# HGRN2 level products of one head: full 128-token blocks, or pairs of 64-column strips

## The chip, the core and the metric

The program runs on one core of a Trainium2 chip. TensorE (PE in the profile, with its weight loads as PEld) multiplies matrices from SBUF into PSUM, VectorE (DVE) and ScalarE (ACT) read and write both, GpSimd (POOL) works in SBUF and issues transfers, and SyncE (SP) issues transfers. Each engine takes its own instructions strictly in a written order and waits on semaphores for the others. The metric is the device time of one execution in microseconds.

## The reference, cut to what matters

Two layers run over 1024 latent tokens (width 1024) behind 256 context tokens. The first mixes neighbourhood attention and mLSTM, and the change does not touch it. The second has 16 bidirectional HGRN2 heads with keys and values of width 128. For one head and one direction:

```
f = lb + (1 - lb) * sigmoid(f_pre);  k = 1 - f;  lf = log(f);  q = silu(q_pre)
b = cumsum(lf)                                          # inside a chunk
o = (q * exp(b)) @ S + sum over s <= t of (q_t . (exp(b_t - b_s) * k_s)) v_s
S = exp(b_last) * S + (k * exp(b_last - b))^T @ v       # carried to the next chunk
```

Both directions are summed, normalised per head, multiplied by silu(z) and projected out. The state S starts from the context tokens.

## The kernel before, in words

Matrix products with weights are made from operands split into a high and a low part, three products each (`dense`, L128 to L130). These carry most of the time of TensorE. In the HGRN2 stage the channels of a head lie on the 128 partitions and tokens run along the columns.

For a head, `hg_proj` makes the forget gates F of both directions and q; `hg_intra` makes the 128 x 128 matrix A of each block of 128 tokens, which holds the weight of token s for token t in both directions; `hg_vz` makes the values v and the gate z, in groups of 24 dense matmuls; `hg_close` transposes the decayed keys; `hg_ctx` makes the starting states from the context; `hg_scan` carries the states over the eight blocks, forms the output of each block from A, q and the states (L1088 to L1090, into PSUM tile acc), and after each four blocks takes the root mean square (squares on ACT at L1104, the power on POOL at L154 and L156) and scales and gates into z (DVE, L1108); `hg_out` transposes z (L1148) and stores it. `wo_sums` and `y_diff` are side work on POOL: they load, add and store pieces of the output weights and of earlier results.

A is built by levels. At level l, with h = 2^l, each pair of neighbouring blocks of h tokens needs the products between its two halves: keys are decayed up to the border between them, queries from it. K and Q hold the keys and queries decayed so far, for both directions; after each level the two halves are multiplied by the totals T of the neighbouring block (DVE, L1048), and the totals are multiplied pairwise (L1050). For the product ACT copies the keys of the right direction into ksel (L1023), TensorE multiplies 128-token blocks (L1028), and DVE writes the part under the level's mask into A (L1037). Everything is done for the two halves of 512 tokens in turn, each with its own tiles. Level 0 and the diagonal are made otherwise: `hg_near` multiplies keys and queries elementwise on DVE, and `hg_close` sums over the channels with a matrix of ones (L998, L999) after a split into two parts, and copies the result to A under a mask (L1001).

What sets the order: the program is written head by head, and a planner with its own costs then lays out each engine's instructions, so that dense products of the next head stand between the level products of this one. The order on each engine is fixed when the kernel is built. PSUM has two banks for dense products (mm), three for level products and states (s), two for transposes (tr) and one for the output (acc). The gate z has one buffer: the next head's z can be written only when this head's transposes have read it, and until then the banks of the dense products that hold it stay in use.

Of the kernel before, what the change touches and what calls it, by code (L numbers as in the profile page):

```python
# [9 lines left out]
F32 = mybir.dt.float32  # L10
# [34 lines left out]
class Prog:  # L45
# [836 lines left out]
    def hg_proj(self, h, pool, w=None):  # L882
# [4 lines left out]
        F = [self.t(p, [P, 2, 512], F32, "gF", 1) for p in (pool, self.fp)]  # L887
# [6 lines left out]
        for d, t0, n in todo:  # L894
            w[d] = w[d] or self.wring([col(1 + d)], P)
            ps = self.ps("mm", [P, n])
            self.proj_tr(ps, w[d], 0, t0, n)
            dst = Fc[:, d, :] if t0 == LAT else F[t0 // 512][:, d, :]
            nc.scalar.activation(dst, ps, AF.Sigmoid)
            nc.vector.tensor_scalar(out=dst, in0=dst, scalar1=olb, scalar2=lb, op0=ALU.mult, op1=ALU.add)  # L900
# [67 lines left out]
    def hg_intra(self, st, pool):  # L968
        nc = self.nc
        n = 512  # L970
        hv = {}
        for hf in (1, 0):
            F, q = st["F"][hf], st["q"][hf]
            K = self.t(pool, [P, 2, n], F32, "gK", 2)
            nc.vector.tensor_scalar(out=K, in0=F, scalar1=-1.0, scalar2=1.0, op0=ALU.mult, op1=ALU.add)
            Q = self.t(pool, [P, 2, n], F32, "gQ", 2)
            for d in range(2):
                nc.vector.tensor_tensor(out=Q[:, 1 - d, :], in0=q, in1=F[:, d, :], op=ALU.mult)
            A = self.t(pool, [P, 4, P], F32, "gA", 2)
            hv[hf] = dict(Q=Q, A=A, T=F, K=K)  # L980
# [7 lines left out]
    def hg_close(self, hv, pool):  # L988
        nc = self.nc
        for i in range(2):  # L990
            for hf in (1, 0):
                H = hv[hf]
# [3 lines left out]
                pa = self.ps("s", [P, 4, P])  # L996
                p2 = pa.rearrange("p a b -> p (a b)")
                nc.tensor.matmul(p2, lhsT=self.ones, rhs=hi, start=True, stop=False)  # L998
                nc.tensor.matmul(p2, lhsT=self.ones, rhs=lo, start=False, stop=True)  # L999
                mask = self.ident8 if i else self.lmask0  # L1000
                nc.vector.copy_predicated(H["A"], mask.unsqueeze(1).to_broadcast([P, 4, P]), pa)  # L1001
        for hf in (1, 0):
            H = hv[hf]
            H["kn"] = []
            for d in range(2):
                p = self.ps("tr", [P, 4, P])
                for c in range(4):
                    nc.tensor.transpose(p[:, c, :], H["K"][:, d, c * P : (c + 1) * P], self.ident)
                k_ = self.t(pool, [P, 512], F32, "gkn", 4).rearrange("p (a b) -> p a b", a=4)
                nc.scalar.copy(k_, p)  # L1010
                H["kn"].append(k_)


    def hg_level(self, H, lev, pool):
        nc = self.nc
        n, h = 512, 1 << lev
        nb = n // (2 * h)
        K, Q, A, Tt = H["K"], H["Q"], H["A"], H["T"]

        pick = lambda t: _skew(t[:, 0, :].rearrange("p (b s i) -> p b s i", s=2, i=h), 2, n)  # L1020
        if lev > 0:
            ksel = self.t(pool, [P, n], F32, "gksel", 3)
            nc.scalar.copy(ksel.rearrange("p (b s i) -> p b s i", s=2, i=h), pick(K))  # L1023
            qp = pick(Q)
            pa = self.ps("s", [P, 4, P])
            nbc = P // (2 * h)
            for c in range(4):
                nc.tensor.matmul(  # L1028
                    pa[:, c, :].rearrange("p (b s i) -> p b s i", s=2, i=h),
                    lhsT=ksel[:, c * P : (c + 1) * P], rhs=qp[:, c * nbc : (c + 1) * nbc], start=True, stop=True,  # L1030
                )
            mask = self.lmask[:, lev - 1, :].unsqueeze(1).to_broadcast([P, 4, P])
            if lev == 1:

                nc.vector.tensor_tensor(out=A, in0=pa, in1=mask, op=ALU.mult)
            elif lev < 6:
                nc.vector.copy_predicated(A, mask, pa)  # L1037
            else:
                nc.scalar.copy(A[0:64, :, 64:P], pa[0:64, :, 64:P])
                nc.scalar.copy(A[64:P, :, 0:64], pa[64:P, :, 0:64])  # L1040
# [8 lines left out]
        Tn = self.t(pool, [P, 2, nb], F32, f"gT{lev}", 2)  # L1049
# [3 lines left out]


    def hg_near(self, H, q, pool):
        nc = self.nc
        n = 512
        K, Q = H["K"], H["Q"]

        kx = bass.AP(K.tensor, K[:, 1, 1:n].offset, [list(K.ap[0]), [2, n // 2], [-(n + 1), 2]])  # L1060
        qx = bass.AP(Q.tensor, Q.offset, [list(Q.ap[0]), [2, n // 2], [n + 1, 2]])
        pr = [self.t(pool, [P, n], F32, "gkn", 4) for _ in range(2)]
        nc.vector.tensor_tensor(out=pr[0].rearrange("p (b s) -> p b s", s=2), in0=kx, in1=qx, op=ALU.mult)
        nc.vector.tensor_tensor(out=pr[1], in0=K[:, 0, :], in1=K[:, 1, :], op=ALU.add)
        nc.vector.tensor_tensor(out=pr[1], in0=pr[1], in1=q, op=ALU.mult)
        H["near"] = pr

    def hg_scan(self, st, halves, S, pool):
# [4 lines left out]
        for c in range(7, 0, -1):  # L1073
            H = halves[c // 4]
            u = self.ps("s", [P, P])
            nc.tensor.matmul(u, lhsT=H["kn"][1][:, c % 4, :], rhs=v[:, c, :], start=True, stop=True)
# [547 lines left out]
```

## Time and profile before

| | us |
|---|---|
| median of 3 runs | 3482.13 (3481.38 to 3482.68) |
| the profiled execution, first to last instruction | 3480.9 |
| PE busy | 3431.2 (99%) |
| PEld busy | 3042.3 (87%) |
| DVE busy | 2307.4 (66%) |
| ACT busy | 1488.6 (43%) |
| POOL busy | 725.6 (21%) |

The profile is of one execution on the hardware. A group of instructions is given with its line, engine, operation, output tile, input tiles, shapes and count; the idle time before it is put down to what ended it. Matmuls are pipelined and their recorded ends are modelled, so starts are the better measure of how long one holds TensorE. A shape "128*64" of a matmul means 128 rows and 64 columns of weights, and "128x128" the moving data. A line of the timeline has the start, the time to the end of its last instruction, and how many instructions it holds.

### The profile page before, as it was taken

The numbers are of one execution on the slowest core, as the hardware profiler recorded it, in microseconds if no ns is written. First come the engines' busy times: TensorE is split into PE (matmuls) and PEld (weight loads), VectorE is DVE, ScalarE is ACT, GpSimd is POOL, SyncE is SP. The second block draws the span as 40 slices with busy tenths as digits, with TensorE's granted clock in tenths as the row PEclk, the third lists the DMA queues.
The fourth block names the chain that finished last, engine by engine and source line by source line (L and its number), as shares of the span: only waits on it lengthen the run. The fifth ranks groups of instructions, "written<-read, shape, count | busy, mean of one in ns | idle before, by whom it ended". The sixth has DMA issues, their size and how long they took to land.

```text
span 3480.9 us, 60852 instructions
## 1 busy us (share of the span) xinstructions
PE 3431.2 (99%) x22668; PEld 3042.3 (87%) x22668; DVE 2307.4 (66%) x5447; ACT 1488.6 (43%) x3577; POOL 725.6 (21%) x1076
## 2 busy tenths in 40 slices
PE   8999999999999999999999999999999999999997
PEld 5779998889989888898888999999999999999876
DVE  4546665666655566787666676667677677666767
ACT  5445554554544444455354333333333333333442
POOL 2222222222111112221110122122223222111125
PEclk9999999999999999999999999999999999999999
DMA  5542222322233434444752111111112211111274
GB/s 205 173 132 59 81 76 74 91 79 75 79 87 99 147 117 127 133 128 148 223 158 68 49 58 55 56 58 58 58 55 64 64 59 57 41 34 34 83 233 154
DMA packets 331527, 333.34 MB, mean 96 GB/s; under 512 B 30984, under 2 KB 277960, under 8 KB 331232
## 3 DMA queue, kind: packets, MB, share of 16 engines
q1 hardware_dynamic: 291008, 222.76, 21.7%
q0 software_dynamic: 40224, 106.69, 9.0%
q8 instruction: 179, 2.93, 0.4%
q14 instruction: 116, 0.95, 0.1%
HBM read 259.40 MB, written 69.79 MB: 95 GB/s over the span
## 4 chain that ended last, share of the span: by engine, by line
PE 89%; DVE 3%; issue 3%; DMA 2%; ACT 1%; POOL 1%; SPq 0%; POOLq 0%; ACTq 0%; DVEq 0%
PE mm L128 18%; PE mm L129 18%; PE mm L130 18%; PE s L1028 5%; PE mm L835 3%; PE mm L836 3%; PE mm L837 3%; PE acc L775 2%; PE tr L755 2%; PE acc L547 2%; PE s L556 2%; PE acc L537 1%; PE acc L1090 1%; PE acc L1088 1%; PE acc L1089 1%
## 5 line engine op out<-in xcount | busy, mean ns | idle before, releaser
L129 PE MATMUL mm<-hl,wh 128*128 128x512 f32 (+1 forms) x1600 | 587.1, 367 | 0.0
L128 PE MATMUL mm<-hh,wh 128*128 128x512 f32 (+1 forms) x1600 | 584.3, 365 | 0.0
L130 PE MATMUL mm<-hh,wl 128*128 128x512 f32 (+1 forms) x1600 | 583.7, 365 | 0.0
L128 PE MATMUL mm<-wh,hh 128*128 128x256 f32 (+1 forms) x1520 | 471.2, 310 | 1.2 <-ACT ev L317 0.6
L129 PE MATMUL mm<-wl,hh 128*128 128x256 f32 (+1 forms) x1520 | 469.9, 309 | 0.0
L130 PE MATMUL mm<-wh,hl 128*128 128x256 f32 (+1 forms) x1520 | 469.0, 309 | 0.3 <-DVE hl L262 0.3
L130 PEld LDWEIGHTS mm<-hh,wl 128*128 128x128 f32 x1600 | 301.6, 189 | 45.0 <-issue 0.5
L128 PEld LDWEIGHTS mm<-hh,wh 128*128 128x128 f32 x1600 | 301.4, 188 | 44.6 <-issue 0.3
L129 PEld LDWEIGHTS mm<-hl,wh 128*128 128x128 f32 x1600 | 301.6, 189 | 43.7 <-issue 0.2
L128 PE MATMUL mm<-wzh,hh 128*128 128x256 f32 x1024 | 299.7, 293 | 2.3 <-DVE gq L909 1.4
L128 PEld LDWEIGHTS mm<-wh,hh 128*128 128x128 f32 x1520 | 286.5, 189 | 16.0 <-issue 1.1
L129 PEld LDWEIGHTS mm<-wl,hh 128*128 128x128 f32 x1520 | 286.5, 188 | 14.7 <-issue 3.0
L130 PEld LDWEIGHTS mm<-wh,hl 128*128 128x128 f32 x1520 | 286.4, 188 | 13.8 <-issue 1.5
L130 PE MATMUL mm<-wzh,hl 128*128 128x256 f32 x1024 | 292.3, 285 | 0.0
L129 PE MATMUL mm<-wzl,hh 128*128 128x256 f32 x1024 | 292.0, 285 | 0.0
L72 ACT CAST wh<-wraw 128x512 fp32r<-128x512 f32 x240 | 147.3, 619 | 233.0 <-PE mm L129 175.8
L73 DVE TENSOR_TENSOR wl<-wraw,wh 128x512 fp32r<-128x512 f32 x240 | 164.8, 691 | 89.6 <-ACT wh L72 80.4
L1023 ACT COPY gksel<-gK 128x512 f32<-128x512 f32 x192 | 120.0, 633 | 218.2 <-PE s L1028 127.3
L1028 PE MATMUL s<-gQ,gksel 128*128 128x128 f32 x1536 | 203.9, 276 | 0.4 <-ACT gksel L1023 0.4
L128 PEld LDWEIGHTS mm<-wzh,hh 128*128 128x128 f32 x1024 | 193.4, 189 | 3.8 <-DVE gq L909 2.4
L129 PEld LDWEIGHTS mm<-wzl,hh 128*128 128x128 f32 x1024 | 193.6, 189 | 0.0
L130 PEld LDWEIGHTS mm<-wzh,hl 128*128 128x128 f32 x1024 | 192.7, 188 | 0.0
(400 smaller groups left out, 8017.5 us busy)
## 6 DMA issues: line engine op xcount, KB each, us to landing
wraw<-in_wab_dram SPq DMA_DIRECT2D x112, 256.0 KB
wraw<-in_wc_dram SPq DMA_DIRECT2D x96, 256.0 KB
wraw<-yd SPq DMA_DIRECT2D x94, 256.0 KB
adar<-in_wada_dram POOLq DMA_DIRECT2D x32, 512.0 KB, 4.4
wraw<-in_wc_dram SPq DMA_DIRECT2D x128, 128.0 KB
md<-ev POOLq DMA_DIRECT2D x60, 256.0 KB, 2.8
mloz<-md SPq DMA_DIRECT2D x40, 256.0 KB
adar<-in_wada_dram SPq DMA_DIRECT2D x16, 512.0 KB
```

The source lines that it names most:

```text
L72: nc.scalar.copy(hi, x)
L73: nc.vector.tensor_tensor(out=lo, in0=x, in1=hi.bitcast(F32), op=ALU.subtract)
L128: mm(ps, lhsT=lh(k), rhs=rh(k), start=(start and k == 0), stop=False)
L129: mm(ps, lhsT=lh(k), rhs=rl(k), start=False, stop=False)
L130: m = mm(ps, lhsT=ll(k), rhs=rh(k), start=False, stop=(stop and k == nk - 1))
L547: nc.tensor.matmul(num, lhsT=qc[:, j, :], rhs=C[d][:, j, :], start=False, stop=(j == 1))
L556: nc.tensor.matmul(u, lhsT=st["k"][c][:, j * P : (j + 1) * P], rhs=vw, start=True, stop=True)
L835: mm(ps, lhsT=yh[k], rhs=w.h(kk), start=(kk == 0), stop=False)
L836: mm(ps, lhsT=yh[k], rhs=w.l(kk), start=False, stop=False)
L837: mm(ps, lhsT=yl[k], rhs=w.h(kk), start=False, stop=(kk == 8 * len(qs) - 1))
L1023: nc.scalar.copy(ksel.rearrange("p (b s i) -> p b s i", s=2, i=h), pick(K))
L1028: nc.tensor.matmul(pa[:, c, :].rearrange("p (b s i) -> p b s i", s=2, i=h), lhsT=ksel[:, c * P : (c + 1) * P], rhs=qp[:, c * nbc : (c + 1) ...
```

## The change

All 1024 tokens of a head are now one piece, with one tile each for F, K, Q and ksel (1024 columns, one buffer) and one chain of levels. Level products are made in blocks of 64 tokens: 64 keys as weights times 64 queries, two such products side by side in the two column halves of TensorE (`strip`, with its tile position), so that the results of 16 blocks fill one PSUM bank of 512 columns. They are gathered in D (128 x 8 x 64) under masks of 64 columns; at level 6, which joins the two 64-token blocks of a pair, D and the level's product are copied into A. The diagonal and level 0, which were elementwise products and column sums with ones, become two more such products: the diagonal of (K0 + K1) with q, and level 0 like the others. `hg_near`, the ones and two masks are gone.

```diff
-        F = [self.t(p, [P, 2, 512], F32, "gF", 1) for p in (pool, self.fp)]
+        F = self.t(self.fp, [P, 2, LAT], F32, "gF", 1)
...
     def hg_intra(self, st, pool):
...
+        K = self.t(pool, [P, 2, LAT], F32, "gK", 1)
+        nc.vector.tensor_scalar(out=K, in0=F, scalar1=-1.0, scalar2=1.0, op0=ALU.mult, op1=ALU.add)
+        Q = self.t(pool, [P, 2, LAT], F32, "gQ", 1)
+        ks = [self.t(pool, [P, 512], F32, "gkn", 4) for _ in range(2)]
         for hf in (1, 0):
...
+            nc.vector.tensor_tensor(out=ks[hf], in0=K[:, 0, s], in1=K[:, 1, s], op=ALU.add)
             for d in range(2):
-                nc.vector.tensor_tensor(out=Q[:, 1 - d, :], in0=q, in1=F[:, d, :], op=ALU.mult)
...
-            self.hg_near(hv[hf], q, pool)
+                nc.vector.tensor_tensor(out=Q[:, 1 - d, s], in0=q[hf], in1=F[:, d, s], op=ALU.mult)
...
+        pa = self.ps("s", [P, 8, 64])
+        for c in range(8):
+            for b in range(2):
+                o = c % 4 * P + b * 64
+                self.strip(pa[:, c, :], b, ks[c // 4][:, o : o + 64], q[c // 4][:, o : o + 64])
+        nc.vector.tensor_tensor(
+            out=hv["D"], in0=pa, in1=self.lmask[:, 0, :].unsqueeze(1).to_broadcast([P, 8, 64]), op=ALU.mult
+        )
         for lev in range(7):
-            for hf in (1, 0):
-                self.hg_level(hv[hf], lev, pool)
+            self.hg_level(hv, lev, pool)
...
+    def strip(self, out, b, lhsT, rhs):
+        s = slice(b * 64, (b + 1) * 64)
+        self.nc.tensor.matmul(out[s], lhsT=lhsT, rhs=rhs, start=True, stop=True, tile_position=(0, b * 64))
...
-    def hg_close(self, hv, pool):
-                hi = self.t(pool, [P, 512], F32R, "gsg", 1)
-                lo = self.t(pool, [P, 512], F32R, "gyt", 1)
-                self.split(hi, lo, H["near"][i])
...
-                nc.tensor.matmul(p2, lhsT=self.ones, rhs=hi, start=True, stop=False)
-                nc.tensor.matmul(p2, lhsT=self.ones, rhs=lo, start=False, stop=True)
...
     def hg_level(self, H, lev, pool):
-        n, h = 512, 1 << lev
+        n, h = LAT, 1 << lev
...
-            ksel = self.t(pool, [P, n], F32, "gksel", 3)
-            nc.scalar.copy(ksel.rearrange("p (b s i) -> p b s i", s=2, i=h), pick(K))
...
-            for c in range(4):
-                nc.tensor.matmul(
-                    pa[:, c, :].rearrange("p (b s i) -> p b s i", s=2, i=h),
-                    lhsT=ksel[:, c * P : (c + 1) * P], rhs=qp[:, c * nbc : (c + 1) * nbc], start=True, stop=True,
-                )
...
+        ksel = self.t(pool, [P, n], F32, "gksel", 1)
+        nc.scalar.copy(ksel.rearrange("p (b s i) -> p b s i", s=2, i=h), pick(K))
+        pa = self.ps("s", [P, 8, 64])
+        for c in range(8):
+            for b in range(2):
...
+                self.strip(out, b, ksel[:, o : o + 64], rhs)
...
+            if lev == 6:
+                nc.scalar.copy(A[s, :, s], D[s])
+                nc.scalar.copy(A[s, :, e], pa[s])
+        if lev < 6:
+            nc.vector.copy_predicated(D, self.lmask[:, lev + 1, :].unsqueeze(1).to_broadcast([P, 8, 64]), pa)
...
-        Tn = self.t(pool, [P, 2, nb], F32, f"gT{lev}", 2)
+        Tn = self.t(pool, [P, 2, nb], F32, f"gT{lev}", 1)
```

The planner lays the instructions out anew in the whole HGRN2 stage; ahead of it and behind it the order stays. In the changed kernel the line numbers shift: its strips are L997, the output products L1073 to L1075 (before L1088 to L1090), the scaling L1093 (L1108), the output transposes L1133 (L1148), the predicated copy L1042 (L1037), the updates of K and Q L1050 (L1048).

On PE, at the end of a head's scan, the four transposes of the second half of its output (tile tr, from gz) stand in the middle of the head behind it. Before, 56 dense matmuls stand between the last output product and this piece:

```order
L128 MATMUL mm_28096<-wzh_27988,hh_20674 128x256
L1148 MATMUL tr_27783<-ident_77,gz_27077 128x128
L924 MATMUL tr_28038<-ident_77,gEc_28036 128x128 x2
L1148 MATMUL tr_27783<-ident_77,gz_27077 128x128
L129 MATMUL mm_28096<-wzl_27987,hh_20674 128x256
L1148 MATMUL tr_27783<-ident_77,gz_27077 128x128
L130 MATMUL mm_28096<-wzh_27988,hl_20675 128x256
```

Now the same transposes, with 22 dense matmuls between the last output product and the strips of level 0:

```order
L130 MATMUL mm_29002<-wzh_28894,hl_20672 128x256
L997 MATMUL s_28724<-gQ_28693,gksel_28722 64x64 x16
L1133 MATMUL tr_28663<-ident_77,gz_27990 128x128
L924 MATMUL tr_28944<-ident_77,gEc_28942 128x128 x2
L1133 MATMUL tr_28663<-ident_77,gz_27990 128x128 x3
L997 MATMUL s_28748<-gQ_28693,gksel_28746 64x64 x16
L128 MATMUL mm_29056<-wzh_28894,hh_20671 128x256
```

The transposes now stand between the strips of level 0 and those of level 1, with no dense matmul among them; nine heads have this piece.

On DVE at the same place, before, the scaling of the output (into gz) stands among the first steps of the half that is not yet at its levels:

```order
L1048 TENSOR_TENSOR gQ_27813<-gQ_27813,gT_5708_27835 128x2x128x2
L978 TENSOR_TENSOR gQ_27824<-gq_27771,gF_27516 128x512 x2
L1063 TENSOR_TENSOR gkn_27828<-gK_27822,gQ_27824 128x512
L1064 TENSOR_TENSOR gkn_27829<-gK_27822 128x512
L1108 SCALAR_TENSOR_TENSOR gz_27077<-acc_27479,gss_27504,gz_27077 128x128 x4
L1048 TENSOR_TENSOR gQ_27824<-gQ_27824,gF_27516 128x2x256
```

Now, with the copy of level 0 (L1042) and the update of Q by level 0 (L1050) behind it:

```order
L979 TENSOR_TENSOR gQ_28693<-gq_28622,gF_28397 128x512 x2
L979 TENSOR_TENSOR gQ_28693<-gq_28651,gF_28397 128x512 x2
L949 TENSOR_SCALAR gq_29193<-gFc_28398 128x512
L1093 SCALAR_TENSOR_TENSOR gz_27990<-acc_28360,gss_28385,gz_27990 128x128 x4
L1042 COPY_PREDICATED gD_28702<-glm_4352_20630,s_28724 128x512
L1050 TENSOR_TENSOR gQ_28693<-gQ_28693,gF_28397 128x2x512
```

All of Q now passes level 0 behind the scaling, where before one half was a level ahead.

On POOL, in the eleventh head, the norm's two steps (gss) stand near the end of two weight sums. Before:

```order
L1125 TENSOR_TENSOR gEc_31552<-gEc_31552,gknc_31551 128x256
L1131 DMA sw_12_74<-gknc_31551 128x256
L1125 TENSOR_TENSOR gEc_31552<-gEc_31552 128x256
L1131 DMA sw_13_75<-gEc_31552 128x256
L1131 DMA sw_14_76<-gEc_31552 128x256
L154 TENSOR_SCALAR gss_31213<-gss_31213 128x4
L156 TENSOR_TENSOR gss_31213<-gss_31213,mhalf_82 128x4
```

Now:

```order
L1110 TENSOR_TENSOR gEc_31478<-gEc_31478,gknc_31477 128x256
L1116 DMA sw_12_74<-gknc_31477 128x256
L154 TENSOR_SCALAR gss_31140<-gss_31140 128x4
L1110 TENSOR_TENSOR gEc_31478<-gEc_31478 128x256
L1116 DMA sw_13_75<-gEc_31478 128x256
L156 TENSOR_TENSOR gss_31140<-gss_31140,mhalf_82 128x4
L1116 DMA sw_14_76<-gEc_31478 128x256
```

The first step of the norm moved ahead of the last sum and its two stores, the second ahead of the last store. Three of the first four output transposes then stand on PE right behind the strips of the diagonal, 124 rows of dense and fp32 products after the context product L961 and those 16 strips.

More of the change, by code (lines that the diff above doesn't have):

```diff
@@ L1048, in hg_level, with hg_scan @@
             nc.vector.tensor_tensor(out=v, in0=v, in1=tot, op=ALU.mult)
-        Tn = self.t(pool, [P, 2, nb], F32, f"gT{lev}", 2)
+        Tn = self.t(pool, [P, 2, nb], F32, f"gT{lev}", 1)
         nc.vector.tensor_tensor(out=Tn, in0=Tv[:, :, :, 0], in1=Tv[:, :, :, 1], op=ALU.mult)
         H["T"] = Tn
[L1055 to L1068, printed above, removed]
+    def hg_scan(self, st, H, S, pool):
         nc = self.nc
@@ L1073, in hg_scan @@
         for c in range(7, 0, -1):
[L1074 removed]
             u = self.ps("s", [P, P])
[L1076 removed]
+            nc.tensor.matmul(u, lhsT=H["kn"][c // 4][1][:, c % 4, :], rhs=v[:, c, :], start=True, stop=True)
             s = self.t(pool, [P, P], F32, "gS1", 10)
             nc.vector.scalar_tensor_tensor(
[L1079 removed]
+                out=s, in0=sb[c], scalar=H["T"][:, 1, c : c + 1], in1=u, op0=ALU.mult, op1=ALU.add
             )
```

80 lines of the change are left out of this document (31 added, 49 removed).

## The prediction

> **What bounds the kernel now.** I read the page first, then the busy time of each engine by stretches, then the groups by line, then the timeline of the places that the change touches.
>
> ```profile
> span 3480.9 us, 60852 instructions
> PE 3431.2 (99%) x22668; PEld 3042.3 (87%) x22668; DVE 2307.4 (66%) x5447; ACT 1488.6 (43%) x3577; POOL 725.6 (21%) x1076
> PEclk9999999999999999999999999999999999999999
> ```
>
> TensorE is busy 99% of the span at full granted clock. A busy TensorE need not be at its peak, but it waits for almost nobody. The HGRN2 stage runs from about 1885 to 3340 us, one head in 90 us; this is one head (columns: stretch, length, then busy time of PE, PEld, DVE, ACT, POOL, clock, DMA share, GB/s):
>
> ```profile
> 2174.00:2264.00 90.00, 90.00 (x628) 83.51 (x627) 62.99 (x121) 32.21 (x76) 18.59 (x27) 1.00 0.18 57
> ```
>
> PE is busy all 90.00 us, DVE 62.99, ACT 32.21, POOL 18.59. So what this stage loses or gains is PE's own work, plus any wait that PE did not have before. The groups that the change touches:
>
> ```profile
> L1028 PE MATMUL s<-gQ,gksel 128*128 128x128 f32 x1536 | 203.9, 276 | 0.4 <-ACT gksel L1023 0.4
> L998 PE MATMUL s<-gsg,ones 128*128 128x512 f32 x64 | 26.6, 415 | 0.0
> L999 PE MATMUL s<-gyt,ones 128*128 128x512 f32 x64 | 25.5, 399 | 0.0
> L1048 DVE TENSOR_TENSOR gK<-gK,gT 128x512 f32<-128x512 f32 x192 | 151.7, 797 | 8.5 <-ACT gksel L1023 8.4
> L1048 DVE TENSOR_TENSOR gQ<-gQ,gT 128x512 f32<-128x512 f32 x192 | 133.3, 694 | 14.3 <-PE s L1028 14.2
> L1023 ACT COPY gksel<-gK 128x512 f32<-128x512 f32 x192 | 120.0, 633 | 218.2 <-PE s L1028 127.3
> ```
>
> The program has 48 level products a head, 768 in all; the trace has 1536 matmuls on L1028. One fp32 product is two records, and prices must be counted in records. What a record occupies is read from the starts:
>
> ```profile
> 2102.22 1.05 PE L1028 MATMUL s<-gQ,gksel 128*128 128x128 f32 x8
> 2103.11 1.04 PE L1008 MATMUL tr<-ident,gK 128*128 128x128 f32 x8
> 2109.53 0.39 PE L128 MATMUL mm<-hh,wh 128*128 128x512 f32 x1
> 2109.76 0.40 PE L129 MATMUL mm<-hl,wh 128*128 128x512 f32 x1
> ```
>
> Eight records take 2103.11 - 2102.22 = 0.89 us, 0.111 each (0.222 an fp32 product); a 512-column matmul of split operands takes 0.23.
>
> **Removed from PE.** 1536 x 0.111 = 170.5 us of level products and 128 x 0.23 = 29.4 us of column sums with the ones (L998, L999): 199.9 us.
>
> **Added to PE.** Eight levels (seven and the diagonal) of 16 strips in 16 heads: 2048 fp32 products of 64 weight columns by 64 moving columns. The nearest row is the attention's product of values, which puts two 64-column strips beside each other in the same way, with 128 moving columns:
>
> ```profile
> 806.50 0.28 PE L130 MATMUL mm<-wh,hl 128*128 128x256 f32 x1
> 806.62 0.28 PE L128 MATMUL mm<-wh,hh 128*128 128x256 f32 x1
> 806.83 0.44 PE L775 MATMUL acc<-apT,avw 128*64 128x128 f32 x4
> 807.10 0.61 PE L775 MATMUL acc<-apT,avc 128*64 128x128 f32 x8
> 807.53 0.61 PE L775 MATMUL acc<-apT,avw 128*64 128x128 f32 x8
> 808.07 0.75 PE L755 MATMUL tr<-ident,aP 128*96 128x128 f32 x5
> 808.58 0.36 PE L707 MATMUL s<-akh,aqs 128*128 128x256 f32 x1
> 808.78 0.28 PE L708 MATMUL s<-akl,aqs 128*128 128x256 f32 x1
> 808.90 0.29 PE L718 MATMUL s<-akh,aqs 128*128 128x264 f32 x1
> 806.83 0.20 PEld L775 LDWEIGHTS acc<-apT,avw 128*64 128x64 f32 x4
> 806.99 0.25 PEld L775 LDWEIGHTS acc<-apT,avc 128*64 128x64 f32 x4
> ```
>
> Eight records from 807.10 to 807.53 are 0.054 each, 0.109 a strip: half of the 0.222 of a full-width product, for half of its work. With 64 moving columns the price lies between 0.109 (nothing gained from fewer columns) and 0.055 (half). The full-width product has weights as wide as its moving data and keeps the rate of one of them, so I go near the lower end; but twice as many instructions must start in a given time as in any row here, so I take 0.060. Sum: 2048 x 0.060 = 122.9 us, and 223.2 at the upper end.
>
> A block of strips has a price of its own. From 806.62 to 808.90 are 2.28 us. The work in it is three matmuls of 256 columns (0.12 each, 806.50 to 806.62), ten strips (1.09) and five transposes (0.10 to 0.11 each): 1.95 to 2.00. So 0.28 to 0.33 us are lost where PE goes over to strips and back; I take 0.30. In the order of the changed kernel the strips stand in 148 blocks, eight to a head and some 20 more because transposes stand between the strips of level 0 in six heads: 148 x 0.30 = 44.4 us. The Trainium skill, "TensorEngine Tiling (Array Packing)", section Key Properties, says that a change of tiling mode drains TensorE, which speaks against short blocks; the 0.28 to 0.33 us agree with it, and a sum that left it out would come 44 us lower.
>
> PE's work: 122.9 + 44.4 - 199.9 = -32.6 us.
>
> **Removed and moved elsewhere.** On DVE the near products, the splits into two parts, half of the predicated copies and the overhead of half of the updates go; per level there remain one update of K and one of Q over 1024 columns (under 2 x 0.797 and 2 x 0.694) and one predicated copy. On ACT the key copy doubles to under 2 x 0.633 and one more per head comes; the near splits go, and four part copies at level 6 stay four, with as many for D. All this costs nothing while PE has other work: between two strip blocks from level 1 on stand 28 to 44 dense matmuls, 4.4 to 6.5 us, against 0.7 + 1.4 + 1.6 = 3.7 us of DVE work a level. Without that cover each level would cost the difference (third rival). One F tile for both halves delays the next head's sigmoids until level 0 is through; they stand behind the key copy of level 5, so nothing. The DMAs are as many as before; a few on POOL and SP change places by one to three rows, and a transfer is issued at most about 2 us earlier or later, in queues that are idle most of the head.
>
> **The wait that comes in.** PE's order is written down, so work taken away brings later instructions forward to data that is not ready. The chain from a head's last output product (L1090) to the transposes of its result (L1148):
>
> ```profile
> 2253.22 0.39 PE L1090 MATMUL acc<-gS,gQ 128*128 128x128 f32 x2
> 2253.71 0.28 ACT L1104 ACTIVATE gjk<-acc 128x128 f32<-128x128 f32 x1 [3.26 <-PE acc L1090]
> 2255.08 0.20 ACT L1104 ACTIVATION_READ_ACCUMULATOR gjk<-acc 128x1 f32 x1
> 2255.37 0.60 POOL L154 TENSOR_SCALAR gss<-gss 128x4 f32<-128x4 f32 x1 [4.01 <-ACT gjk L1104]
> 2256.05 1.65 POOL L156 TENSOR_TENSOR gss<-gss,mhalf 128x4 f32<-128x4 f32 x1
> 2257.74 1.13 DVE L1108 SCALAR_TENSOR_TENSOR gz<-acc,gss,gz 128x128 f32<-128x128 f32 x4 [0.33 <-POOL gss L156]
> 2258.78 0.68 DVE L1048 TENSOR_TENSOR gQ<-gQ,gF 128x512 f32<-128x512 f32 x1
> 2260.17 0.27 PE L1148 MATMUL tr<-ident,gz 128*128 128x128 f32 x1
> ```
>
> The first scaled block is there 2257.74 + 0.35 - 2253.22 = 4.9 us after the product, the fourth after 5.65. Before, PE reaches the transposes after 6.95 us (2260.17) and never waits. In nine heads of the changed kernel only 22 dense matmuls (2.6 us) and the 16 strips of level 0 (16 x 0.06 + 0.3 = 1.26) stand there: PE arrives after 0.22 + 2.6 + 1.26 = 4.1 us. Behind the transposes stand, with nothing between, the strips of level 1. They need Q updated by level 0, and on DVE the predicated copy and that update stand behind the scaling: 5.65 + 0.66 (512 columns: 0.69 busy, begun just before the operation ahead ends) + 1.15 (an estimate for 1024 columns from the same rows) = 7.5 us. Without a wait PE would be there after 4.1 + 0.65 = 4.75. That is 2.8 us of wait, and 0.3 for the same chain at the first four transposes: 9 x 3.1 = 27.9 us. Who waits behind PE: the dense matmuls of the next group, whose PSUM banks come free only after these transposes, since the gate tile z has one buffer; so nothing can fill it.
>
> In the eleventh to thirteenth heads another chain ends last. There POOL makes two weight sums after the context product L961, before the norm:
>
> ```profile
> 2756.72 1.05 PE L961 MATMUL s<-gv,gknc 128*128 128x128 f32 x8
> 2774.45 0.56 POOL L1131 DMA_DIRECT2D sw<-gknc  x1
> 2775.04 0.75 POOL L1125 TENSOR_TENSOR gEc<-gEc 128x256 f32<-128x256 f32 x1
> 2786.29 0.42 POOL L154 TENSOR_SCALAR gss<-gss 128x4 f32<-128x4 f32 x1 [9.48 <-ACT gjk L1104]
> 2786.80 1.53 POOL L156 TENSOR_TENSOR gss<-gss,mhalf 128x4 f32<-128x4 f32 x1
> ```
>
> In the new order L154 stands behind the store of 2774.45, ahead of one more sum (0.75) and store (0.6). It starts when its product is through, 18.2 us after L961 by the order, plus 2.1: 20.3; then 0.3 + 0.75 + 0.6 + 1.5 = 23.5, scaled blocks 1 to 3 by 24.55. PE arrives 72 x 0.118 + 23 x 0.231 + 29 x 0.222 + 1.26 = 21.5 us after L961 and has three transposes in a row: 2.8 us of wait, 3 x 2.8 = 8.5. The tenth head has 0.7 by the same working. For the first, second and last heads, which have other neighbours, I put 4 us as an estimate from the same steps (in the last one the strips of levels 4 and 5 stand side by side, 2 us). Waits together: 27.9 + 8.5 + 0.7 + 4 = 41 us.
>
> **The sum.** -32.6 + 41 = +8.4: 3480.9 + 8.4 = 3489.3 us of span. The median of the runs shown, 3482.13, stands 1.2 over this execution's span, so 3490.5; I predict 3491. Both ends stay: strips at 0.055 give 10 us less.
>
> **Rivals.** First, the waits are hidden: the chain ends earlier or PE's other losses push the transposes back. Then only the work counts: 3482.1 - 32.6 = 3449. For it: each loss ahead of the transposes shortens the wait by as much. Against: PE's rows there leave 4.1 us for a chain of 4.9.
>
> Second, fewer moving columns bring nothing: 2048 x 0.049 = 100 us more, less 0.8 x 2 x 9 = 14 by which the waits shorten: 3577. It decides from 0.075 a strip on. For it: no row has a shorter moving side than 128. Against: the rows of L775 show loads of the next strips (806.99) running beside matmuls that started at 806.83 and 807.10. The Trainium skill, "TensorE: Matmul & The Clock Gate", section What overlaps and what doesn't, says that a weight load overlaps matmuls in flight only when the row groups differ. Both strips use all rows here, so by that rule load and matmul would follow each other and this rival would be right; the 0.054 a record disagrees with it.
>
> Third, the levels become the bound: with one chain for all tokens, DVE's 3.7 us and its other work of that stretch (scans, splits, lower bounds) exceed PE's cover by 1 us at five levels in 16 heads: 80 us more, 3571. Against: before, DVE has 27 of 90 us free, and the change takes work from it.
>
> Fourth, going over to strips costs 0.6, since a block of short matmuls hides less of it: 44 more, 5 less wait: 3530.
>
> **How the numbers follow.** About 0.2% (7 us) is what a measurement of this kernel tells from no change. Forecast 0.52, with an own range of 3475 to 3512 (strips 0.055 to 0.065, loss 0.25 to 0.35, waits half an order of their size off); first rival 0.20, second 0.10, third 0.08, fourth 0.10. Range 3447 to 3555: it takes in the first and fourth rival and leaves out the second and third, and some tails, about 0.2. Faster than 3475: the first rival and a little of the forecast, 0.23. Within 7 us: the lower part of the forecast, 0.20. Slower: the rest, 0.57.
>
> **What would show it.** In the profile of the changed kernel the strips' line should hold 4096 records at starts 0.03 us apart on average; a level's 16 strips and the step back should take 1.2 to 1.3 us. PE should show idle time, ended by the DVE scaling at the output transposes and by DVE's Q at the strips, of some 40 us where it now has almost none; DVE should fall by over 10 us a head. The prediction is wrong if a strip takes 0.075 or more, if the idle time is under 10 or over 70 us, or if dense matmuls fill the place between levels 0 and 1.

## The result, and the profile after

The changed kernel takes 3486.11 us (median of 19 runs, 3478.37 to 3489.91); the kernel before, run beside it, 3482.68 (19 runs, 3479.62 to 3486.51). The ratio is 1.0005, 95% interval 0.9999 to 1.0011: no change that this measurement can tell. The prediction was 3491, inside a range of 3447 to 3555; the largest chance stood on "slower by over 0.2%", which did not come.

The page of the changed kernel's profiled execution, the lines that answer to those of before:

```profile
span 3488.0 us, 64893 instructions
PE 3409.5 (98%) x25100; PEld 2990.6 (86%) x25100; DVE 2098.0 (60%) x4855; ACT 1478.0 (42%) x3433; POOL 707.3 (20%) x1076
PEclk9999999999999999999999999999999999999999
```

TensorE is busy 21.7 us less than before in a span that is 7.1 us longer. So it now waits. The busy time by stretches (length, then PE, PEld, DVE, ACT, POOL, clock, DMA share, GB/s), first one head, then the HGRN2 stage:

```profile
2174.00:2264.00 90.00, 88.44 (x790) 80.48 (x789) 51.64 (x86) 32.29 (x70) 19.75 (x28) 1.00 0.18 57
...
1885.00:3345.00 1460.00, 1431.33 (x12482) 1290.91 (x12481) 827.72 (x1355) 522.32 (x1087) 275.48 (x382) 0.99 0.18 57
```

The stage in the kernel before:

```profile
1885.00:3345.00 1460.00, 1455.44 (x10046) 1345.12 (x10045) 1030.03 (x1933) 531.15 (x1229) 284.86 (x384) 1.00 0.18 58
```

TensorE's idle time in these 1460 us went from 4.6 to 28.7 us. DVE lost 11.4 us in the 90 us shown, and nobody gained from it. Read from one last output product to the next, a head in the middle of the stage (third to eighth) went from 90.03 to 88.95 us, 1.56 of which are idle time: 2.64 us of work less, 1.08 of length. The tenth to thirteenth went the other way, from 90.5 to 90.8 us before to 92.5 to 93.1.

**The strips cost what was forecast.** The groups hold 3584 + 512 = 4096 records on L997. One block in the timeline of the changed kernel:

```profile
2363.57 0.28 PE L129 MATMUL mm<-wzl,hh 128*128 128x256 f32 x1
2363.78 1.15 PE L997 MATMUL s<-gQ,gksel 128*64 128x64 f32 x32
2364.86 0.38 PE L130 MATMUL mm<-wzh,hl 128*128 128x256 f32 x1
2365.08 0.28 PE L128 MATMUL mm<-wzh,hh 128*128 128x256 f32 x1
```

From 2363.57 to 2365.08 are 1.51 us, with two matmuls of 0.12 in them: 1.27 for 16 strips and the going over. Level 0 is dearer: from its strips to the next instruction TensorE takes 1.49 us (2353.54 to 2355.03 in the rows below), where levels 2 to 6 and the diagonal take 1.08 (2363.78 to 2364.86) and level 1 about 1.13. Why was not tried.

**Where TensorE waits.** The waits of PE (engine, line, who released it: us in total, times, longest):

```profile
PE s L997 <- DVE gQ L1050: 14.4, 10, 1.5
PE tr L1133 <- DVE gz L1093: 6.3, 4, 1.9
PE s L997 <- ACT gksel L1024: 2.4, 1, 2.4
PE s L997 <- DVE gQ L979: 1.7, 1, 1.7
```

Both places that the prediction named are there. The first of them, in the timeline of all engines:

```profile
2350.47 0.39 PE L1075 MATMUL acc<-gS,gQ 128*128 128x128 f32 x2
...
2352.62 0.22 POOL L154 TENSOR_SCALAR gss<-gss 128x4 f32<-128x4 f32 x1 [2.54 <-ACT gjk L1089]
2352.93 1.36 POOL L156 TENSOR_TENSOR gss<-gss,mhalf 128x4 f32<-128x4 f32 x1
...
2353.54 1.56 PE L997 MATMUL s<-gQ,gksel 128*64 128x64 f32 x32
2354.32 1.13 DVE L1093 SCALAR_TENSOR_TENSOR gz<-acc,gss,gz 128x128 f32<-128x128 f32 x4 [0.59 <-POOL gss L156]
2355.03 0.33 PE L1133 MATMUL tr<-ident,gz 128*128 128x128 f32 x1
...
2355.20 0.38 PE L924 MATMUL tr<-ident,gEc 128*128 128x128 f32 x2
2355.36 0.72 DVE L1042 COPY_PREDICATED gD<-glm,s 128x512 f32<-128x512 uint8 x1
2355.41 0.49 PE L1133 MATMUL tr<-ident,gz 128*128 128x128 f32 x3
2355.98 1.21 DVE L1050 TENSOR_TENSOR gQ<-gQ,gF 128x1024 f32<-128x1024 f32 x1
...
2357.33 1.18 PE L997 MATMUL s<-gQ,gksel 128*64 128x64 f32 x32 [1.43 <-DVE gQ L1050]
```

The output transposes (2355.03) find their data; the strips of level 1 (2357.33) wait 1.43 us for DVE's update of Q, which stands behind the scaling.

The second place is the output transposes in the three heads where the prediction saw POOL's weight sums ahead of the norm (counted by output products they are the tenth to twelfth, by strips the eleventh to thirteenth). POOL's rows in the first of them show the norm cut in two by the second weight sum: L154, then a sum and a store, then L156.

```profile
2789.61 0.19 POOL L154 TENSOR_SCALAR gss<-gss 128x4 f32<-128x4 f32 x1 [1.85 <-ACT gjk L1089]
2789.88 0.73 POOL L1110 TENSOR_TENSOR gEc<-gEc 128x256 f32<-128x256 f32 x1
2790.55 0.59 POOL L1116 DMA_DIRECT2D sw<-gEc  x1
2791.17 1.03 POOL L156 TENSOR_TENSOR gss<-gss,mhalf 128x4 f32<-128x4 f32 x1
```

**What nobody had put in the sum.** The same place, 1 us at a time (the number before the DMA share is the granted clock):

```profile
2791.00:2792.00 1.00, 0.00 (x0) 0.00 (x0) 0.60 (x1) 0.00 (x0) 0.97 (x2) 1.00 0.30 123
2792.00:2793.00 1.00, 0.27 (x2) 0.24 (x2) 0.76 (x3) 0.00 (x0) 0.76 (x2) 1.00 0.03 8
2793.00:2794.00 1.00, 0.98 (x8) 0.76 (x8) 0.36 (x2) 0.00 (x0) 0.00 (x0) 1.00 0.32 131
2794.00:2795.00 1.00, 1.00 (x8) 1.00 (x7) 0.35 (x1) 0.37 (x1) 0.00 (x0) 0.52 0.00 0
2795.00:2796.00 1.00, 1.00 (x6) 1.00 (x6) 0.15 (x1) 0.00 (x0) 0.00 (x0) 0.50 0.00 0
...
2797.00:2798.00 1.00, 1.00 (x9) 1.00 (x9) 0.00 (x0) 0.60 (x1) 0.10 (x1) 0.77 0.00 0
```

TensorE stands from 2790.86 to 2792.73 (1.87 us). From 2794.04 to 2797.45, 3.41 us, it is granted half its clock: an fp32 product then takes 0.43 us (2794.32 to 2794.75 in the timeline) in place of 0.22. That costs another 1.7 us after the wait is over. It happens in each of these three heads, once in the fourteenth (behind waits of 1.74 and 1.50 us), and twice in a row in the last, behind a wait of 2.42 us: 6 x 1.7 = 10.2 us in the stage, where the kernel before had none. The nine waits of 1.43 to 1.45 us are followed by no such stretch. The Trainium skill, "TensorE: Matmul & The Clock Gate", section What's actually happening, has the clock set by a free-running window of 3413 ns; the 3.41 us agree. The Trainium skill's advice to avoid idle gaps over about 3 us (same page, section Why this matters for your kernels) is too mild for this trace: 1.87 us were enough, three times out of three.

So the account of the stage is, as an estimate: 16 heads x 2.64 us of work less is 42; 20 blocks that are cut apart by transposes give some 6 or 7 back; waits give 24 back, the halved clock 10. That leaves -2, against +3 measured by the medians and +7 in the two profiled executions. The 7 us of the profiled executions arise ahead of the stage. Up to 1885 us TensorE's order is the same in both kernels, and still the same matmul stands at 1851.04 us before and at 1858.19 us in the changed kernel; from there to the end both take as long, within 0.1 us, which is near the -2 of the account. The largest part arises where TensorE waits for ACT (yh), and ACT for loads; first before, then in the changed kernel:

```profile
1740.44 0.50 PE L835 MATMUL mm<-woh,yh 128*128 128x512 f32 x1 [0.99 <-ACT yh L72]
```

```profile
1746.63 0.79 PE L835 MATMUL mm<-woh,yh 128*128 128x512 f32 x1 [3.22 <-ACT yh L72]
```

In the ten profiles of kernels with the change this wait is 1.3 to 4.5 us long, in the two without it 0.9 and 1.0, and the matmul of 1851.04 us comes 2 to 9 us later than in the profile before. Why, no run here shows, nor how much of the +3 of the medians it is.

### The profile page after: what moved, and what is told of

Read it like the earlier page. It is cut to its first block, busy times and chain, and to the rows that moved or that the text cites. A ratio compares the mean times of both kernels' runs of the same rounds, so it can differ in the third digit from the quotient of the medians.

```text
span 3488.0 us, 64893 instructions
## 1 busy us (share of the span) xinstructions
PE 3409.5 (98%) x25100; PEld 2990.6 (86%) x25100; DVE 2098.0 (60%) x4855; ACT 1478.0 (42%) x3433; POOL 707.3 (20%) x1076
## 4 chain that ended last, share of the span: by engine, by line
PE 85%; DMA 4%; issue 3%; DVE 3%; POOL 2%; ACT 1%; SPq 0%; POOLq 0%; DVEq 0%; ACTq 0%
PE mm L128 18%; PE mm L129 18%; PE mm L130 18%; PE s L997 4%; PE acc L775 2%; PE mm L837 2%; PE mm L835 2%; PE mm L836 2%; PE tr L755 2%; PE acc L547 2%; PE s L556 2%; PE acc L537 1%; PE tr L1009 1%; PE acc L1073 1%; PE acc L1074 1%
## 5 line engine op out<-in xcount | busy, mean ns | idle before, releaser
L1024 ACT COPY gksel<-gK 128x1024 f32<-128x1024 f32 x112 | 128.0, 1143 | 213.0 <-PE s L997 139.2
L835 PE MATMUL mm<-woh,yh 128*128 128x512 f32 x422 | 170.4, 404 | 9.8 <-DVE og L1366 5.2
```

Source lines behind the costliest of these rows:

```text
L835: mm(ps, lhsT=yh[k], rhs=w.h(kk), start=(kk == 0), stop=False)
```

## The experiments

All are edits of the changed kernel, unless said otherwise. Ratios are to the kernel before, with 95% intervals.

**1. Full-width products in the compact form.**

```
-        pa = self.ps("s", [P, 8, 64])
...
+        for hf in (1, 0):
+            pa = self.ps("s", [P, 4, P])
+            for c in range(4):
+                g = hf * 4 + c
+                nc.tensor.matmul(
+                    pa[:, c, :].rearrange("p (b s i) -> p b s i", s=2, i=h),
+                    lhsT=ksel[:, g * P : (g + 1) * P], rhs=qp[:, g * nbc : (g + 1) * nbc], start=True, stop=True,
+                )
...
```

> Strips alone undone: everything else of the changed kernel stays (one key copy, one update of K and Q over 1024 tokens, near products as two more levels), but each level is again eight full-width products of 128 by 128 in two banks, copied into A under a mask of 128 columns. First theory (16 strips with the going over cost 1.27 us, as read in the changed kernel's trace, eight products cost 8 x 0.222 = 1.78): 8 levels x 16 heads x 0.51 = 65 us more of TensorE's work, less some 6 us because the longer level 0 shortens the wait behind it: about 3486 + 59 = 3545 us. Second theory (a strip is no cheaper than its share of a full-width product, and the changed kernel's level work is saved elsewhere): no change, 3486. Against the kernel before it also shows what the compact form costs without strips: about 60 us.

Measured: 3550.16 us, ratio 1.0195 (1.0180 to 1.0210), 64 more than the changed kernel. The first theory's time holds: strips alone are worth 64 us here. That it lies so near is partly luck. A head in the middle now has 5.4 us more of TensorE's work (93.59 with 0.79 of idle time, against 88.95 with 1.56), 87 in 16 heads and not 65; among other things, the products of level 0 take 2.66 us (2372.16 to 2374.82) in place of the 1.78 reckoned. Some 19 of the 87 are hidden, since the stage has 18.2 us of idle time in place of 28.7 and one stretch of halved clock in place of six. The rest of the change alone, two more levels in place of the column sums among it, costs about 67 against the kernel before, 14 of them as waits.

**2. The strips in another order.**

```
-        for c in range(8):
-            for b in range(2):
+        for b in range(2):
+            for c in range(8):
```

> The 16 strips of a level in another order: first the eight of columns 0 to 63, then the eight of columns 64 to 127, in place of alternating. First theory (a strip's weights load beside the matmul before it only because that one uses the other half of the columns): seven of eight strips lose the overlap, up to 0.109 in place of 0.06 each, 2048 x 0.875 x 0.049 = 88 us more, 3574. Second theory (loads run beside matmuls whatever columns they use): within 5 us of the changed kernel, 3486.

Measured: 3576.15 us, 1.0270 (1.0255 to 1.0286), 90 more. The same 16 strips:

```profile
2400.68 1.90 PE L997 MATMUL s<-gQ,gksel 128*64 128x64 f32 x32
2402.51 0.38 PE L128 MATMUL mm<-wzh,hh 128*128 128x256 f32 x1
```

1.83 us to the next matmul in place of 1.08 (2363.78 to 2364.86): 0.047 more a strip, so 0.107 in place of 0.061. A strip is cheap because the next one uses the other 64 columns. But it is not the weight load alone that this hides, as the first theory has it. In the changed kernel the records start in pairs, 7 ns apart, with a pair every 58 ns (2363.942 and 2363.949, then 2364.001 and 2364.007), and their weight loads do so too; in this order one record starts every 58 ns (2400.841, 2400.899, 2400.958). Two strips on different halves multiply side by side. The 0.107 agrees with the price of the prediction's second rival, but it has another cause: 64 columns of weights and of queries do take half of the 0.222 of a full-width product, and what is lost is the other half's work at the same time. The Trainium skill, "TensorE: Matmul & The Clock Gate", section What overlaps and what doesn't, lets a weight load overlap matmuls in flight only where the row groups differ. The row groups are the same in both orders, so that rule does not tell the two apart, which differ by 90 us.

**3. One weight sum a head on POOL.**

```
-                    for i in ([h] if h < 8 else [2 * h - 8, 2 * h - 7] if h < 12 else []):
+                    for i in ([0, 1] if h == 0 else [h + 1] if h < 15 else []):
```

> POOL makes one weight sum a head (two in the first), not two in the ninth to twelfth; nothing else is changed, and TensorE's order in the tenth to thirteenth heads becomes that of the others. First theory (the wait of 1.87 us at the output transposes there comes from the second sum standing ahead of the norm on POOL, and the granted clock of 0.50 over 3.41 us comes from that wait; with the level-0 strips cut into five blocks they make these heads 92.5 us long where the others have 88.94): 3 x 3.6 + 2.9 for the tenth + 1.9 for the fourteenth, whose extra stall goes too: 15 us less, about 3471, and no stretch of halved clock from 2000 to 3250 us. Second theory (these heads are longer for another reason than POOL's order): 3486, with the clock drops still there.

Measured: 3475.24 us, 0.9979 (0.9970 to 0.9989), 10.9 less than the changed kernel. The tenth to fourteenth heads are now 88.93 us like the others, and no halved clock is left between 2000 and 3250 us: the first theory's cause holds. The edit also takes 15 cuts out of the strips (133 blocks in place of 148), so the share of the wait alone is not told apart. In the two profiled executions these five heads are 16.8 us shorter, the last head is 4.5 longer, and the whole is 15 us shorter, as forecast; by the medians 4 of these are missing, and no run tells where. TensorE stands 2.96 us in the last head, against 2.42 in the changed kernel, and 4.15 behind it.

**4. A longer wait.** Level 0's strips follow the output transposes (the other edits let `strip` return its matmul and keep the last transpose):

```
-                self.strip(out, b, ksel[:, o : o + 64], rhs)
+                m = self.strip(out, b, ksel[:, o : o + 64], rhs)
+                if lev == 0 and self.last:
+                    self.behind(m, self.last)
```

> Level 0's 16 strips are made to follow the output transposes on TensorE, which takes them (and some of the dense matmuls) out of the place ahead of these transposes: in most heads only 8 dense matmuls are left there, and TensorE arrives about 1.2 us after the last output product, where the chain of squares, norm and scaling needs 4.6 us by the changed kernel's trace. The waits at level 1 go, since 37 dense matmuls now stand there. First theory (idle time alone counts): 3.4 in place of 1.56 us in 11 heads, 20 us more; 3506. Second theory (idle time of more than about half of a 3.41 us window also halves the granted clock for the next 3.41 us): in addition 1.7 us, at most 3.4, in each of these heads, 19 to 37 us: 3525 to 3543, with 11 or more stretches of clock 0.50. Third theory (the waits are not what holds the changed kernel back): within 5 us of 3486.

Measured: 3513.27 us, 1.0088 (1.0071 to 1.0105), 27 more. The longest sum of PE's waits in the stage, and one head 1 us at a time, during its wait (2174, 2176) and behind it (2178):

```profile
PE tr L1135 <- DVE gz L1095: 39.3, 14, 3.4
```

```profile
2174.00:2175.00 1.00, 0.08 (x1) 0.00 (x0) 1.00 (x3) 0.90 (x5) 0.00 (x0) 1.00 0.00 0
...
2176.00:2177.00 1.00, 0.00 (x0) 0.00 (x0) 0.07 (x2) 0.00 (x0) 0.90 (x1) 1.00 0.00 0
...
2178.00:2179.00 1.00, 1.00 (x11) 0.74 (x12) 1.00 (x5) 0.71 (x2) 0.00 (x0) 0.50 0.03 8
```

Idle time rose by 20.0 us, as both theories had it. Nearly every head now has its 3.41 us of halved clock: 14 windows of that length in place of 6, 13.7 us more. 21 fewer blocks at 0.3 take 6 off: 20 + 14 - 6 = 28. The second theory's stretches of halved clock came, so idle time alone does not count; but the time is below its 3525 to 3543, since one window a head is all that comes, and since it left the fewer blocks out.

**5 to 7. A second buffer for z.**

```
-        z = self.t(pool, [P, NT - 2, P], F32, "gz", 1)
+        z = self.t(pool, [P, NT - 2, P], F32, "gz", 2)
...
-        Tn = self.t(pool, [P, 2, nb], F32, f"gT{lev}", 1)
+        Tn = self.t(pool, [P, (LAT, 512)[lev % 2]], F32, f"gT{lev % 2}", 1)[:, 0 : 2 * nb].rearrange("p (d b) -> p d b", d=2)
```

> The gate tile z gets a second buffer (room for it is made by letting the chunk products T of the levels share two tiles), so that the next head's v and z matmuls need not wait for the output transposes: TensorE's order now has 44 dense matmuls ahead of them in place of 22, and 35 between levels 0 and 1. But the order also cuts level 0's strips into five blocks by the transposes in nearly all heads: 186 blocks in place of 148. First theory (the waits cost 23 us of idle time and 10 of halved clock, and each cut of a block costs 0.65 us, which is 9.7 us over the 15 blocks that one sum a head saved): -33 + 38 x 0.65 = -8: 3478 us. Second theory (a cut costs 0.3, as the prediction had it): 3465. Third theory (the waits are not what holds the changed kernel back): 3486 or more.

Measured: 3487.69 us, 1.0011 (1.0002 to 1.0020). The waits at level 1 are gone, but for one in the last head: idle time in the stage fell from 28.7 to 13.5 us, and one of six windows of halved clock is left. The time did not fall with them. The cut blocks take a part of it: the seventh and eighth heads, without idle time, take 89.15 us, and 87.67 with four cuts fewer in the next experiment, 0.37 a cut, which is some 14 us for 38. The price of 0.65, from which I had 3478, was wrong. By these numbers the time should have fallen by 10 us, and it rose by 2: some 11 us are not settled.

With level 0's strips behind the transposes, by the edit of experiment 4:

> Two buffers for z as above, and level 0's strips made to follow the output transposes, so that they stand in one block (129 blocks in all): no wait at the transposes, no wait at level 1, no cut. First theory (waits, halved clock and cuts are what took back the strips' gain): 3486 - 33 + 6 for what is left of idle time - 19 x 0.65 = 3447 us, that is 1.0% under the kernel before, with under 12 us of idle time and at most two stretches of halved clock between 1885 and 3345 us. Second theory (the strips gain nothing, the waits only hide it): 3480 or more.

Measured: 3467.84 us, 0.9957 (0.9943 to 0.9970). 57 blocks fewer than the one before and 19.9 us less: 0.35 for each cut. The heads in the middle are 87.67 us long, without idle time. But 3447 was not reached: the stage still has 15.6 us of idle time and five windows of halved clock, where under 12 and at most two were forecast. PE's waits in the stage begin with

```profile
PE tr L1135 <- DVE gz L1095: 6.7, 2, 3.6
```

which are the output transposes of the last head, with the halved clock behind them: the dense work that the second buffer lets TensorE draw ahead may have been the last head's cover (experiment 9 tries it).

With the diagonal's strips behind the transposes too (the same two lines at the diagonal):

> As the one with whole blocks, and the diagonal's strips too are made to follow the output transposes, so that they stand beside level 0's: blocks of 32 strips, 113 blocks in place of 129. First theory (going over to strips and back costs 0.30 us a block): 16 x 0.30 = 5 us less than with blocks of 16, about 3442, and a block of 32 strips takes 0.30 + 32 x 0.06 = 2.2 us. Second theory (the loss comes with every strip, not with the block): the same time as with blocks of 16, and 2.5 us a block.

Measured: 3475.55 us, 0.9980 (0.9971 to 0.9989). The undisturbed heads (sixth to eighth) fell from 87.67 to 87.37: 0.30 us for one block fewer, the first theory's price. Two levels' strips side by side show what a strip costs without the going over:

```profile
2437.79 1.15 PE L999 MATMUL s<-gq,gkn 128*64 128x64 f32 x32
2438.77 1.51 PE L999 MATMUL s<-gQ,gksel 128*64 128x64 f32 x32
2440.22 0.39 PE L130 MATMUL mm<-wzh,hl 128*128 128x256 f32 x1
```

0.98 us from one 16 to the next: 0.061 a strip. The whole kernel, however, is 8 us slower than with blocks of 16, and 3442 was missed: from the ninth head on most heads have waits of about 1 us again, once or twice, and the ninth to fourteenth are 90.4 to 92.2 us long.

**8. Merged blocks and one sum a head.** Experiments 3 and 7 together.

> The one with merged blocks, and one weight sum a head on POOL. First theory (what POOL's second sum delays is the norm, and with two z buffers 18 to 39 more dense matmuls, 2 to 4.6 us, cover that): within 4 us of the one with merged blocks. Second theory (the norm still comes late in the tenth to thirteenth heads): 5 to 8 us less.

Measured: 3465.21 us, 0.9949 (0.9936 to 0.9961), 10.3 less than with merged blocks: the second theory, and more than it said. Heads eleven to fifteen are 87.8 us. The 6.7 us at the last head's transposes are still there.

**9. Cover for the last head.** Of the output projection that fills the last head, two tiles follow its fourth and eighth output product:

```
-                self.out_part(w, 0, 0, S, yp, lambda t, ps: add(u[:, t, :], ps, p[:, t, :]))
+                self.out_part(w, 0, 0, S, yp, lambda t, ps: add(u[:, t, :], ps, p[:, t, :]), late={2: self.prod[3], 3: self.prod[7]})
...
+                if late and k == 0:
+                    self.behind(m, late)
```

> Two z buffers, merged blocks and one sum a head, and in addition two of the eight token tiles of the output projection that fill the last head (24 matmuls of 512 columns each, 24 x 0.23 = 5.5 us) are made to follow that head's fourth and eighth output products, so that TensorE has work where the one before stood 3.09 and 3.59 us at the last output transposes. First theory (dense work drawn ahead by the second z buffer is missing as cover in the last head): 6.7 us of idle time go, and with them most of the 7 us that the halved clock costs from 3310 to 3335 us: 8 to 13 us less than 3465, about 3455. Second theory (the stall only moves on, to the loads of the final stage): within 3 us of 3465.

Measured: 3449.79 us, 0.9908 (0.9893 to 0.9923): faster than both kernels, by 0.9% against the kernel before the change, and 15.4 us less than experiment 8, where 8 to 13 were forecast. It was the last head's cover: the wait for gz is gone. (Of the 19.2 us between the profiled executions of the two, 7.1 arise ahead of the stage, where their order is the same.) The stage in this kernel has 12.4 us of idle time and two stretches of halved clock, both in or behind the last head:

```profile
1885.00:3345.00 1460.00, 1447.63 (x12608) 1307.76 (x12607) 833.68 (x1391) 531.21 (x1108) 276.99 (x393) 1.00 0.21 64
```

**10. The kernel before with one sum a head** (the edit of experiment 3 there).

> The kernel before the change with one weight sum a head (two in the first) and nothing else, to see what of the gains of the last kernels has nothing to do with strips. By the heads' lengths before the change (90.5 to 90.8 us in the tenth to fourteenth, 92.7 in the ninth, against 90.03 in the others, with 0.27 us of idle time) at most 5 us are to be had: first theory 3478 to 3483 us; second theory (POOL's second sum costs the kernel before as much as the changed one): 3472.

Measured: 3479.04 us, 0.9989 (0.9981 to 0.9998): 3.5 us, the first theory. Of the last kernel's 33 us, about 29 are therefore not due to the weight sums. That they belong to strips that nothing has to wait for is argued: the second z buffer and the cover for the last head were not tried on the kernel before. Its stage has 4.6 us of idle time and no halved clock, so there is little for them to take.

## Why the prediction was right or wrong

- **TensorE's work was right.** A strip was taken at 0.060 and is 0.061; going over to strips was taken at 0.30 and is 0.30 for a whole block (0.35 where a block is cut). Sixteen strips and the step back were to take 1.2 to 1.3 us and take 1.27, but for level 0, which the working had not set apart and which takes about 0.4 more.
- **That DVE's and ACT's savings bring nothing was right.** DVE fell by 11.4 us in 90, and no level after level 1 makes TensorE wait for it.
- **That waits would take the gain back was right in kind, place and cause**: one z buffer, with nothing to fill the gap (experiments 5 and 6 take the waits away by a second one), and POOL's second sum (experiment 3).
- **The term that failed is the size and make-up of the waits, 41 us.** Nine heads were to lose 3.1 us each and lost 1.4 at level 1, 1.6 in all. The chain was 0.8 us shorter than the rows of before gave: POOL's norm took 1.67 us (2352.62 to 2354.29) in place of 2.33, and Q was updated 6.7 us after the output product in place of 7.5. Why POOL was quicker was not tried. And TensorE came 0.7 later: level 0's strips took 1.49 us in place of 1.26 and began 0.25 later, so that the transposes started after 4.56 us in place of 4.1, and two of the next head's v (L924), which the working left out, stand among them. Both errors made the wait too long. In the three heads with POOL's second sum the wait was 1.87 in place of 2.8. The fourteenth head has two waits that no term named, 3.2 us together. In all the stage's idle time grew by 24 us.
- **A term was missing: the halved clock**, 10 us in the stage. It made up for part of the overestimate, so the sum (+8.4 forecast, +3.4 measured by the medians) looks better than its parts. In the profiled executions the stage and what follows it cost nothing, and all of the 7 us more arise ahead of it, in no term of the sum. That 3491 lies so near to 3486 is partly luck.
- **The rivals.** Waits hidden, 3449: not in this kernel. That experiment 9 reached 3449.79 once most of them were gone is a coincidence of the number, since it also has 36 blocks fewer and one weight sum a head. Strips at 0.109: wrong here. The prediction's reason for the low price, that weights and moving data shrink together, holds for half of the way, from 0.222 to 0.107; the other half, to 0.061, comes from strips on different columns side by side, as in the rows of L775 from which the price was taken. What spoke against this rival in the prediction, that weight loads run beside matmuls, is so in both orders and does not decide. And that no row of before has a shorter moving side than 128 overlooks L194: with 128 columns of weights and 2 moving ones its records start every 0.112 us (21.552, 21.664), as with 128, so beside wide weights fewer moving columns do bring nothing. Levels bound by DVE, and a going over of 0.6: neither.
- **The chances.** 0.57 on slower came from an own range placed around a sum that was 5 us too high; a change of 3 us lies below what can be told.

## What to carry to other kernels

Price work taken off a busy engine together with the cover that it gave: some 42 us of TensorE's work were saved in the stage, and nearly the whole came back as waits of 1.4 to 2.4 us, as cut blocks and as halved clock. Give the late result a second buffer and keep a block of strips whole, alternate the columns of neighbouring strips, and see who covers the last pass of a loop from which work is drawn ahead. Count a wait of TensorE near 2 us as two: its own length, and up to 1.7 us of halved clock behind it. Compare a change in one stage with a matmul ahead of it, too: here what differed in the profiles lay there.

## What the runs showed of the hardware that was not expected

- Two 64-column strips on alternating columns: 0.061 us each, started in pairs 7 ns apart. The same strips in runs on the same columns: 0.107.
- Sixteen strips of level 0, whose queries are every second column of Q, take 1.49 us to the next instruction; those of levels 2 to 6 take 1.08. In the order of experiment 2 these are 2.49 and 1.83, for the full-width products of experiment 1 2.66 and 1.70. Why was not tried.
- Mixing strips into full-width work costs 0.30 us a block, whether of 16 or 32 strips, and about 0.35 for each cut through a block.
- An idle stretch of 1.87 us (three of three), and 12 of the 14 of 2.3 to 3.4 us in experiment 4, were followed by 3.41 us at half the granted clock; the nine of 1.43 to 1.45 us were not. One of 2.98 us in the kernel before, ahead of this stage, was not either, so length alone does not decide. The traces show what does. In each of the twelve the stretches of halved clock begin on a grid of 3.413 us, within 0.01 us. Counting TensorE's idle time inside each window of that grid that has the full clock, from 150 us on to 20 us before the end: with 1.8 us or more the next window was halved 67 times out of 67, with 1.5 to 1.8 us 9 times out of 34, with less never (over 11000 windows). The 1.87 us all lie in one window; the 2.98 us are cut into 1.74 and 1.23, and the two exceptions of experiment 4 into 1.34 and 1.20, and 1.64 and 0.79. No run moved a wait within its window on purpose.
